# A decoder layer in fp32 products of split operands: the last output part rebuilt, copies of x shared out, and two attention-side products put in another order

## The chip, the cores and the metric

The kernel runs on one core of one Trainium2 chip. The metric is the device time of one execution in microseconds (us), lower being better. TensorE is called PE here, VectorE DVE, ScalarE ACT, GpSimd POOL and SyncE SP; PEld is PE's weight loading.

## The reference

One decoder layer on x of 512 rows by 1024, with a memory of 256 rows:

```python
x = x + 0.5 * swiglu(rms_norm(x, norm_ffn1_w), ffn1_w_in, ffn1_w_out)     # "ffn1", d_ff 2816
x = x + hybrid_mixer(rms_norm(x, norm_mix_w), ...)   # SSD scan heads + differential attention
x = x + memory_cross_attention(rms_norm(x, norm_cross_w), rms_norm(mem, norm_mem_w), ...)
x = x + 0.5 * swiglu(rms_norm(x, norm_ffn2_w), ffn2_w_in, ffn2_w_out)     # "ffn2"
return rms_norm(x, norm_final_w)

def swiglu(h, w_in, w_out):
    gate, up = jnp.split(h @ w_in, 2, axis=-1)
    return (jax.nn.silu(gate) * up) @ w_out
```

Two inner products matter below. In the differential attention the weights `w = softmax0 - lam * softmax1` are multiplied by the values, one head at a time (`po` in the kernel). In the scan the decayed products of a chunk are `y_diag` and `y_off` (`pf`, then `py` in the kernel). Both sums and products are over fp32 data.

## The kernel before, in words

**Split operands.** Every fp32 operand of a large product is split into a high and a low half. ACT copies the high half (line 155, tiles `wh`, `s31h` and so on), DVE subtracts it from the operand to get the low half (line 156, `wl`, `s31l`). A product is then three matmuls: high by high, low by high, high by low. The line numbers 155 and 156 are those of the helper, so they are the same for all tiles.

**The two feed-forward parts** use a Strassen-like scheme: for a block of four quarters, seven products instead of eight, on sums S1 to S4 of the quarters. The sums of the activations are built in `block_sums` (lines 212 to 214): `s` (the sum s31), then two half-width subtractions and additions that make the sum s24 of it, then the splits. The output product (`out_blocks`, from line 1285) runs in three sets over the 22 blocks of d_ff: 6, 8 and 8 for the first layer part. A set runs seven products of 24 matmuls of 128x512: `11` into `oa`, S1 into `oe` (these two in turn, part by part), S2 into `ob`, `12` into `oa`, S3 into `ob`, S4 into `oe`, `22` into `ob`. Each needs two parts of weights, 128x1024 each. Where the product's weights are themselves sums of quarters, the sum is made on the chip: a fetch (SP) and an accumulating DMA (POOL, line 1345), or an addition on DVE (line 1355, `t2`).

The third set of ffn1 is built with `by_dma`: its weight sums come in while the set runs. Its second product (`oe`) needs S1's weight parts and `s31l`. Next to it in PE's order stands `prel`, two 256-wide products of the relative-position bias, whose result ACT copies (`hot`, line 640) and stores by two DMAs of its own queue (`rel_d`, line 643).

**What sets the order.** SP and POOL work in the order in which the program writes their instructions. The order of ACT, DVE and PE comes from a scheduler; in the program, `Order` steps through generators whose `yield` values are the time until the next piece is due, and `behind(...)` holds an instruction after named others. Every queue then runs in order: an instruction that waits holds all behind it.

**Buffers.** Fetched weights (`wr`) have six buffers, high and low halves (`wh`, `wl`) three each. The eight PSUM banks are `acc` (4) and `aux` (4).

**Other places.** `turn` (line 1249 on) transposes four tiles of x on PE into four banks (`pxf`) and copies each back on ACT (line 1258), between ffn1 and the mixer. `memory_in` (line 1069) splits the memory's tiles (`hm`). `head` computes `po`, and `group` computes `pf` and `py`.

Of the kernel before, what the change touches and what calls it, by code (L numbers as in the profile page):

```python
# [11 lines left out]
F32 = mybir.dt.float32  # L12
R32 = mybir.dt.float32r
AF = mybir.ActivationFunctionType
ALU = mybir.AluOpType
# [85 lines left out]
def body(tc, a, dbg=None):  # L101
# [37 lines left out]

    last, start, last_sum, recent, newest, newest_mm, first_block = [], [], [], [], [], [], []  # L140
    V, S, G = nc.vector, nc.scalar, nc.gpsimd
# [63 lines left out]
    def sums_in_steps(b11, b21, b22, b12, pair=None):  # L205

        s31, s24 = s2("s31"), s2("s24")
        if pair is None:
            V.tensor_tensor(s31[:, :H], b11, b21, ALU.subtract)
            V.tensor_tensor(s31[:, H:], b21, b22, ALU.subtract)  # L210
        else:
            V.tensor_tensor(halves(s31), *pair, ALU.subtract)  # L212
        V.tensor_tensor(s24[:, :H], s31[:, H:], b11, ALU.subtract)
        V.tensor_tensor(s24[:, H:], s24[:, :H], b12, ALU.add)  # L214
        s31 = split("s31", s31)
        yield
        s24 = split("s24", s24)
        lo, hi = slice(0, H), slice(H, T)
        yield {S3: hl(s31, lo), S1: hl(s31, hi), S2: hl(s24, lo), S4: hl(s24, hi)}
# [546 lines left out]
    def head(hd, q, kq, bias):  # L766
# [69 lines left out]
        po = aux("po")  # L836
        for j in range(4):
            mm3(po[:, j * P :], v[j], (w0[j], w1[j]), j == 0, j == 3, wc=hs)
        w0.clear()
# [87 lines left out]
    def group(g, bt, ct, xs, zs):  # L927
# [52 lines left out]
        for j in range(2):  # L980
# [14 lines left out]
            with behind(list(newest_mm)):  # L995
                for c in range(1, 4):
                    mm(pf[:, c * P : (c + 1) * P], st[c - 1][:, j * P : (j + 1) * P], ct[:, c * P : (c + 1) * P], True, True)
                for c in range(4):
                    for hh in range(2):
                        pp = slice(64 * hh, 64 * hh + 64)  # L1000
                        mm(py[pp, c * P : (c + 1) * P], xdt[c // 2][:, c % 2, (2 * j + hh) * 64 : (2 * j + hh + 1) * 64], rs[hh][:, c], True, True)
# [67 lines left out]
    def memory_in(dst):  # L1069
        yield 9.0  # L1070
        for k in range(KT):
            mk = mem[k // 2][:, k % 2]
            with behind(recent):
                dst.append(split("hm", mk, par[:, C_MEM + k : C_MEM + k + 1], True))
            yield 2.0
        mem.clear()
        both = small("nboth", 4, bufs=2)[:, :2]
        V.tensor_tensor(both, msq[:, :2], msq[:, 2:], ALU.add)
        yield from st_mem.from_sums(both, 10.0)
# [171 lines left out]
    def turn(n, banks=None, summed=False):  # L1251
# [5 lines left out]
        for tb in range(4):  # L1257
            S.activation(x[4 * n + tb], pt[tb], AF.Copy)
            if summed:
# [27 lines left out]
    def out_blocks(blocks, sums, g, col4, ncol4, each=None, finale=None, clean=True, n=None, by_dma=False):  # L1287
# [13 lines left out]

        def weights(of, part, raw=None):
            if raw is None:
# [3 lines left out]
            lo = wp.tile([P, w], R32, tag="wl", name=nm("wl"))  # L1307
            recent[:] = [i.ins for i in split_into(hi, lo, raw)]
            return hi, lo
# [12 lines left out]
        def product(ps, of, which, first=False, ready=None, after=((), ())):  # L1322
            for part in parts:
                if ready and part == parts[0]:
                    w = ready
                else:
# [26 lines left out]
        def t2(part):  # L1353
            more = fetch(blocks[B22], part)
            V.tensor_tensor(t_raw[part], t_raw[part], more, ALU.add)
            return t_raw[part]
# [10 lines left out]

        later = {}
        here = sums is None
        if here:  # L1370
            sums = [t1, added(blocks[B12], blocks[B22], "gate"), t2, lambda part: t_raw[part]]
        ready = [None, None]
        if early:
            ready = [weights(of, parts[0]) for of in (blocks[B11], sums[0])]
            yield
        bank = [acc, aux]
# [5 lines left out]
        both = [product(a_ps, blocks[B11], "11", True, ready[0]), product(e_ps, sums[0], S1, True, ready[1], ((), tuple(first_block)))]  # L1382
        for _ in parts:
# [23 lines left out]
        for n, _ in enumerate(product(b_ps, sums[1], S3, after=(copies, ()))):  # L1407
            if n == 0:
                first_split = list(recent)
            elif n == 12 and by_dma:  # L1410
                with behind(first_split):
                    for part in t_raw:
                        t4(part)
            yield
        for t in range(2):
# [181 lines left out]
```

## Time and profile before

| | us |
|---|---|
| time, median of 3 runs (1299.22 to 1300.01) | 1299.35 |
| profiled execution: its own time | 1299.78 |
| profiled execution: span | 1298.0 |
| PE busy | 1284.4 |
| PEld busy | 1125.5 |
| DVE busy | 970.5 |
| ACT busy | 710.2 |
| POOL busy | 119.1 |
| third output set of ffn1, first product to last | 300.04 to 342.49 |
| transposes of x after it (`pxf`) | from 342.49 |

PE is busy for nearly the whole span, so time is only to be had where PE stands idle or runs below its usual pace: the list of waits gives the first, the start times of neighbouring matmuls in the timeline the second. In a timeline row, the first number is the start, the second the time from the start to the end of the row's group, `x4` the number of instructions in the group, and the brackets hold the idle time before it with what ended it. Rows of matmuls overlap by some tenths, since their ends are modelled. In rows of the windows view the columns are the stretch, its length, busy time of PE, PEld, DVE, ACT and POOL (with instructions), then the granted clock of PE as a share of full speed, the share of time of the DMA engines, and GB/s.

### The profile page before, as it was taken

To read this page: it belongs to the slowest core of one execution; us is meant where nothing else is said; L and a number is where in the kernel's file an instruction comes from. 1 tells how busy PE (TensorE), PEld (TensorE's weight loads), DVE (VectorE), ACT (ScalarE), POOL (GpSimd) and SP (SyncE) were. 2 spreads that over 40 slices of the span, in tenths; PEclk is the share of its full clock that TensorE was granted. 3 is DMA by queue.
4 is the path that set the end of the run, shared out by engine and by line. 5 is a ranking of instruction groups with operands and counts; after the bars stand their busy time and mean duration, and the time that the engine had idled before them with its cause. 6 is when DMAs were issued, how large, how long until landed. Compare 5 with 4: busy or idle time off the path is not lost.

```text
span 1298.0 us, 20081 instructions
## 1 busy us (share of the span) xinstructions
PE 1284.4 (99%) x7709; PEld 1125.5 (87%) x7709; DVE 970.5 (75%) x1543; ACT 710.2 (55%) x1207; POOL 119.1 (9%) x149
## 2 busy tenths in 40 slices
PE   9999999999999999999999999999999999999997
PEld 7889998998888778877888888889899899989995
DVE  6988897797776676567867696645678878877886
ACT  7544564565654564346644574434466546555554
POOL 1001010001101011100102011020001000000000
PEclk9999999999999999999999999999999999999999
DMA  9468777777975436653475567693249876666662
GB/s 336 101 172 209 183 195 207 227 192 203 295 234 155 131 65 159 227 165 98 106 207 180 158 163 223 198 228 113 66 130 249 214 223 183 185 191 191 173 206 94
DMA packets 69264, 234.75 MB, mean 181 GB/s; under 512 B 8161, under 2 KB 9665, under 8 KB 68817
## 3 DMA queue, kind: packets, MB, share of 16 engines
q1 hardware_dynamic: 53200, 180.91, 41.8%
q0 software_dynamic: 13168, 45.67, 19.8%
q10 hardware_dynamic: 2800, 6.91, 1.6%
q8 instruction: 60, 0.98, 0.3%
q14 instruction: 36, 0.29, 0.1%
HBM read 231.30 MB, written 48.29 MB: 215 GB/s over the span
## 4 chain that ended last, share of the span: by engine, by line
PE 81%; issue 12%; DMA 2%; DVE 2%; POOL 1%; ACT 1%; POOLq 0%; SPq 0%; ACTq 0%; DVEq 0%
PE qb L242 11%; PE pm L146 10%; PE qe L242 8%; PE qa L242 8%; PE pxbc L146 5%; PE ob L1319 5%; PE oa L1319 4%; PE pcq L146 3%; PE oe L1319 3%; PE pz L146 3%; PE pk L146 2%; PE pq L146 2%; PE pa L146 2%; PE pcv L146 2%; PE pv L146 2%
## 5 line engine op out<-in xcount | busy, mean ns | idle before, releaser
L155 ACT ACTIVATE wh<-wr 128x1024 fp32r<-128x1024 f32 (+1 forms) x323 | 328.2, 1018 | 304.6 <-PE qe L242 37.2
L156 DVE TENSOR_TENSOR wl<-wr,wh 128x1024 fp32r<-128x1024 f32 (+1 forms) x323 | 378.4, 1175 | 99.7 <-ACT wh L155 73.0
L788 ACT ACTIVATE ec<-ec,mn 128x512 f32<-128x512 f32 (+3 forms) x64 | 35.4, 554 | 22.0 <-DVE mn L787 22.0
L787 DVE CUSTOM_DVE_ANT_0 ec<-ps,bias 128x512 f32<-128x512 f32 (+3 forms) x64 | 28.1, 487 | 16.1 <-PE ps L146 15.9
L900 DVE SCALAR_TENSOR_TENSOR conv<-pxbc,par,conv 128x511 f32<-128x511 f32 (+2 forms) x48 | 35.7, 744 | 3.5 <-ACT conv L896 2.9
L251 POOL DMA_DIRECT2D wr<-in_f2q x11 | 9.7, 879 | 307.7 <-DMA wr<-in_f2q 116.8
L366 POOL TENSOR_TENSOR ncol<-nv,mhalf 128x4 f32<-128x4 f32 (+1 forms) x9 | 11.0, 1222 | 291.1 <-DVE nv L364 291.1
L146 PE MATMUL pxbc<-hnl,wh 128*128 128x512 f32 x128 | 35.6, 404 | 0.0
L146 PE MATMUL pxbc<-hnh,wh 128*128 128x512 f32 x128 | 35.3, 400 | 0.0
L146 PE MATMUL pxbc<-hnh,wl 128*128 128x512 f32 x128 | 32.3, 393 | 0.0
L453 DVE TENSOR_TENSOR gate<-qb,row 128x512 f32<-128x512 f32 x19 | 13.1, 692 | 22.1 <-PE qb L242 22.1
L146 PEld LDWEIGHTS pxbc<-hnh,wl 128*128 128x128 f32 x128 | 23.8, 188 | 5.3 <-issue 0.2
L251 POOL DMA_DIRECT2D wr<-in_f1q x16 | 14.0, 873 | 152.2 <-DMA wr<-in_f1q 58.9
L146 PEld LDWEIGHTS pxbc<-hnl,wh 128*128 128x128 f32 x128 | 23.2, 188 | 4.7 <-issue 0.4
L146 PEld LDWEIGHTS pxbc<-hnh,wh 128*128 128x128 f32 x128 | 23.0, 189 | 4.6 <-issue 0.5
L454 ACT ACTIVATE gate<-gate 128x1024 f32<-128x1024 f32 x19 | 20.1, 1057 | 10.9 <-DVE gate L453 10.9
L146 PE MATMUL pv<-wh,hnh 128*128 128x512 f32 x64 | 25.3, 395 | 0.0
L146 PE MATMUL pv<-wh,hnl 128*128 128x512 f32 x64 | 25.2, 393 | 0.0
L855 POOL TENSOR_TENSOR rr<-ev,mhalf 128x4 f32<-128x4 f32 x8 | 8.3, 1034 | 163.1 <-DVE ev L853 163.1
L155 ACT ACTIVATE s31h<-s 128x512 fp32r<-128x512 f32 x30 | 18.7, 624 | 7.4 <-DVE s L212 4.4
L155 ACT ACTIVATE s24h<-s 128x512 fp32r<-128x512 f32 x30 | 18.8, 625 | 7.0 <-DVE s L214 7.0
L301 ACT ACTIVATE u<-qb 128x512 f32<-128x512 f32 x19 | 11.4, 598 | 19.8 <-PE qb L242 19.8
(461 smaller groups left out, 3527.9 us busy)
## 6 DMA issues: line engine op xcount, KB each, us to landing
wr<-in_f2q SPq DMA_DIRECT2D x44, 512.0 KB, 4.4
wr<-in_f1q SPq DMA_DIRECT2D x40, 512.0 KB, 4.3
wr<-in_f1b SPq DMA_DIRECT2D x25, 512.0 KB, 5.3
isum<-in_f2q SPq DMA_DIRECT2D x22, 512.0 KB, 5.4
wr<-isum SPq DMA_DIRECT2D x22, 512.0 KB, 4.2
wsum<-in_f2b SPq DMA_DIRECT2D x20, 512.0 KB, 6.3
wr<-wsum SPq DMA_DIRECT2D x20, 512.0 KB, 4.4
wr<-in_f1q POOLq DMA_DIRECT2D x16, 512.0 KB, 6.5
```

The source lines that it names most:

```text
L146: newest_mm[:] = [nc.tensor.matmul(out, w, x, start=start, stop=stop).ins]
L155: S.activation(hi, src, AF.Copy),
L156: V.tensor_tensor(lo, src, hi.bitcast(F32), ALU.subtract),
L242: newest_mm[:] = [nc.tensor.matmul(out, w_[:, wc], xs[kp][which][x_], start=first and j == 0 and f == 0 and kp == 0, stop=j == 2 and kp == ...
L251: last_sum[:] = [G.dma_start(raw, m, accum_op=ALU.add).ins]
L301: copy = S.activation(u2, b_ps, AF.Copy)
L453: V.tensor_tensor(gate[:, 2 * i : 2 * i + 2], halves(gs[i]), row, ALU.mult)
L454: S.activation(gate, gate, AF.Silu)
L787: V.tensor_tensor_reduce(out=ec[:, :n], in0=ps[c][:, parts[i]], in1=bias[:, T - n :], scale=0.125, scalar=3e38, op0=ALU.add, op1=ALU.min, ...
L788: S.activation(ec[:, :n], ec[:, :n], AF.Exp, bias=mn, scale=-1.0, accum_out=sm[c][:, i : i + 1])
L900: V.scalar_tensor_tensor(y[:, d:], ps[:, : T - d], par[:, cw + j : cw + j + 1], y[:, d:], ALU.mult, ALU.add)
L1319: newest_mm[:] = [nc.tensor.matmul(ps, a_[:, ts], b_[:, ws], start=first and k == 0 and j == 0, stop=k == n - 1 and j == 2, skip_group_che ...
```

## The change

It has six parts.

1. In every set, the low split of the first part of S2's weights is held behind the low split of s31 (`sums_low`); all of S2's weight splits are written ahead of the copies of `oa` into `ob` (line 1392 before), and in the third set the updates of x from `oe` come behind those splits.
2. In the third set (`by_dma`) the new `ask_early` fetches B11's and S1's second part, then B22 in four 128x512 pieces named `more` (two 128x1024 fetches before), and then both parts of S3, first the `wr` buffer and then the spare `gate`, ahead of B21. The two DVE additions of t2 become four of 128x512. The accumulating DMAs of t4 go out half way through product `12` and not S3's.
3. `memory_in` starts later: its first yield is 13, not 9.
4. In `turn`, when called with banks of its own, the odd tiles' copies of x go to DVE (4 of 8).
5. In `head` the order is all `(high value, first weights)`, all `(low value, first weights)`, all `(high value, second weights)`, the last in the order 1, 2, 3, 0; before, the three stood together per tile.
6. In `group` the two halves of `py` come in the order (1, 0), not (0, 1).

```diff
@@ block_sums
         s31 = split("s31", s31)
+        sums_low[:] = last[1:]
         yield
         s24 = split("s24", s24)
@@ head
-        for j in range(4):
-            mm3(po[:, j * P :], v[j], (w0[j], w1[j]), j == 0, j == 3, wc=hs)
+        for n, (v_, w_) in enumerate(((0, w0), (1, w0), (0, w1))):
+            for j in (0, 1, 2, 3) if n < 2 else (1, 2, 3, 0):
+                mm(po[:, j * P :], v[j][v_][:, hs], w_[j], n + j == 0, n == 2 and j == 0)
@@ group
-                    for hh in range(2):
+                    for hh in (1, 0):
@@ memory_in
-        yield 9.0
+        yield 13.0
@@ turn
         for tb in range(4):
-            S.activation(x[4 * n + tb], pt[tb], AF.Copy)
+            if banks and tb % 2:
+                V.tensor_copy(x[4 * n + tb], pt[tb])
+            else:
+                S.activation(x[4 * n + tb], pt[tb], AF.Copy)
@@ weights
-            recent[:] = [i.ins for i in split_into(hi, lo, raw)]
+            high = S.activation(hi, raw, AF.Copy)
+            with behind(low_behind):
+                low = V.tensor_tensor(lo, raw, hi.bitcast(F32), ALU.subtract)
+            recent[:] = [high.ins, low.ins]
@@ t2
-            more = fetch(blocks[B22], part)
-            V.tensor_tensor(t_raw[part], t_raw[part], more, ALU.add)
+            more = pieces.pop(part) if part in pieces else (fetch(blocks[B22], part),)
+            n = t_raw[part].shape[1] // len(more)
+            for i, m in enumerate(more):
+                V.tensor_tensor(t_raw[part][:, i * n : (i + 1) * n], t_raw[part][:, i * n : (i + 1) * n], m, ALU.add)
@@ out_blocks
+        def ask_early():
+            for of, make in ((B11, lambda part: fetch(blocks[B11], part)), (S1, t1)):
+                asked[of, parts[1]] = make(parts[1])
+            for part in parts:
+                pieces[part] = [s2("more") for _ in range(*part)]
+                for k, m in zip(range(*part), pieces[part]):
+                    nc.sync.dma_start(m, blocks[B22][:, k * T : (k + 1) * T])
+            for part in parts:
+                asked[S3, part] = seventh(part)
...
         u2 = []
+        third = {part: weights(sums[2], part, low_behind=() if n else sums_low) for n, part in enumerate(parts if by_dma else parts[:1])}
+        third_split = list(recent) if by_dma else []
         for t in range(2):
             S.activation(b_ps[t], a_ps[t], AF.Copy)
-        for t in range(2):
-            update(t + 2, 1, e_ps[t], 1, False)
-        yield from product(b_ps, sums[2], S2)
+        with behind(third_split):
+            for t in range(2):
+                update(t + 2, 1, e_ps[t], 1, False)
+        yield from product(b_ps, sums[2], S2, ready=third)
...
-        yield from product(a_ps, b21 if here and not by_dma else blocks[B21], "12")
+        for n, _ in enumerate(product(a_ps, b21 if here and not by_dma else blocks[B21], "12")):
+            if n == 12 and by_dma:
+                for part in t_raw:
+                    t4(part)
+            yield
```

How this stands in the engines' order, at three places of the third set of ffn1. First ACT, from the high half of S1's second weights to the splits after `hot`, before the change (`wh` first is S1's second part, `wh` second is S2's first part):

```order
L155 ACTIVATE wh_3462<-wr_3459 128x1024
L155 ACTIVATE s31h_3396<-s_597_3391 128x512
L155 ACTIVATE wh_3495<-wr_3373 128x1024
L155 ACTIVATE s24h_3400<-s_598_3392 128x512
L1392 ACTIVATE ob_3412<-oa_3408 128x512
L1392 ACTIVATE ob_3413<-oa_3409 128x512
L155 ACTIVATE gh_3404<-th_3381 128x512
L640 ACTIVATE hot_2459<-prel_3473 8x256
L640 ACTIVATE hot_2460<-prel_3473 8x256
L643 DMA rel_d<-hot_2459 8x256
```

and after it:

```order
L1313 ACTIVATE wh_3476<-wr_3410 128x1024
L155 ACTIVATE s31h_3396<-s_597_3391 128x512
L155 ACTIVATE s24h_3400<-s_598_3392 128x512
L155 ACTIVATE gh_3404<-th_3381 128x512
L1421 ACTIVATE ob_3431<-oa_3427 128x512
L1421 ACTIVATE ob_3432<-oa_3428 128x512
L641 ACTIVATE hot_2459<-prel_3487 8x256
L641 ACTIVATE hot_2460<-prel_3487 8x256
L644 DMA rel_d<-hot_2459 8x256
L644 DMA rel_d<-hot_2460 8x256
L1313 ACTIVATE wh_3501<-wr_3373 128x1024
L1313 ACTIVATE wh_3507<-wr_3410 128x1024
```

The high half of S2's first part (`wh_3495`, now `wh_3501`) moved from the third row of the first list to behind the copies of `oa`, both `hot` copies and both DMAs.

DVE at the same place, before:

```order
L156 TENSOR_TENSOR wl_3463<-wr_3459,wh_3462 128x1024
L213 TENSOR_TENSOR s_598_3392<-s_597_3391,th_3381 128x256
L1355 TENSOR_TENSOR wr_3373<-wr_3373,wr_3492 128x1024
L214 TENSOR_TENSOR s_598_3392<-s_598_3392,th_3381 128x256
L156 TENSOR_TENSOR s31l_3397<-s_597_3391,s31h_3396 128x512
L1355 TENSOR_TENSOR wr_3459<-wr_3459,wr_3516 128x1024
L156 TENSOR_TENSOR s24l_3401<-s_598_3392,s24h_3400 128x512
L156 TENSOR_TENSOR wl_3496<-wr_3373,wh_3495 128x1024
L156 TENSOR_TENSOR gl_3405<-th_3381,gh_3404 128x512
```

and after:

```order
L1315 TENSOR_TENSOR wl_3477<-wr_3410,wh_3476 128x1024
L213 TENSOR_TENSOR s_598_3392<-s_597_3391,th_3381 128x256
L214 TENSOR_TENSOR s_598_3392<-s_598_3392,th_3381 128x256
L156 TENSOR_TENSOR s31l_3397<-s_597_3391,s31h_3396 128x512
L156 TENSOR_TENSOR s24l_3401<-s_598_3392,s24h_3400 128x512
L156 TENSOR_TENSOR gl_3405<-th_3381,gh_3404 128x512
L1365 TENSOR_TENSOR wr_3373<-wr_3373,more_3413 128x512
L1365 TENSOR_TENSOR wr_3373<-wr_3373,more_3414 128x512
L1365 TENSOR_TENSOR wr_3410<-wr_3410,more_3417 128x512
L1365 TENSOR_TENSOR wr_3410<-wr_3410,more_3418 128x512
L1315 TENSOR_TENSOR wl_3502<-wr_3373,wh_3501 128x1024
```

The 128x1024 addition that stood between the sums and `s31l` is behind it now, in four pieces, and with it the other addition.

SP, the fetches of the third set from S1's second part (`wr_3459`, now `wr_3410`) on, before (`wr_3492` and `wr_3516` are B22, `wr_3544` and `wr_3568` B21, `wr_3591` and `gate` S3):

```order
L1299 DMA wr_3459<-in_f1b 128x1024
L1299 DMA wr_3492<-in_f1b 128x1024
L1299 DMA wr_3516<-in_f1b 128x1024
L1299 DMA wr_3544<-in_f1b 128x1024
L1299 DMA wr_3568<-in_f1b 128x1024
L1299 DMA wr_3591<-in_f1b 128x1024
L1299 DMA gate_3617<-in_f1b 128x1024
```

and after:

```order
L1304 DMA wr_3410<-in_f1b 128x1024
L1386 DMA more_3413<-in_f1b 128x512
L1386 DMA more_3414<-in_f1b 128x512
L1386 DMA more_3417<-in_f1b 128x512
L1386 DMA more_3418<-in_f1b 128x512
L1304 DMA wr_3421<-in_f1b 128x1024
L1304 DMA gate_3424<-in_f1b 128x1024
L1304 DMA wr_3553<-in_f1b 128x1024
L1304 DMA wr_3574<-in_f1b 128x1024
```

S3's two fetches moved ahead of B21's two, and B22 comes in four pieces.

More of the change, by code (lines that the diff above doesn't have):

```diff
@@ L138, in dump @@
             nc.sync.dma_start(dbg[name], t.bitcast(F32) if t.dtype == R32 else t)
-    last, start, last_sum, recent, newest, newest_mm, first_block = [], [], [], [], [], [], []
+    last, start, last_sum, recent, newest, newest_mm, first_block, sums_low = [], [], [], [], [], [], [], []
     V, S, G = nc.vector, nc.scalar, nc.gpsimd
@@ L1300, in fetch, with weights @@
             return raw
-        def weights(of, part, raw=None):
+        def weights(of, part, raw=None, low_behind=()):
             if raw is None:
@@ L1323, in product @@
             for part in parts:
-                if ready and part == parts[0]:
-                    w = ready
+                if ready and part in ready:
+                    w = ready[part]
                 else:
@@ L1366, in t4, with early_or @@
             G.dma_start(t_raw[part], blocks[B21][:, part[0] * T : part[1] * T], accum_op=ALU.add)
-        later = {}
+        later, pieces, asked = {}, {}, {}
+        def ask_early():
[7 more added lines that the diff above has]
+                asked[S3, part] = seventh(part)
+        def early_or(of, make):
+            return lambda part: asked.pop((of, part)) if (of, part) in asked else make(part)
         here = sums is None
         if here:
-            sums = [t1, added(blocks[B12], blocks[B22], "gate"), t2, lambda part: t_raw[part]]
+            seventh = added(blocks[B12], blocks[B22], "gate")
+            sums = [early_or(S1, t1), early_or(S3, seventh), t2, lambda part: t_raw[part]]
         ready = [None, None]
         if early:
-            ready = [weights(of, parts[0]) for of in (blocks[B11], sums[0])]
+            ready = [{parts[0]: weights(of, parts[0])} for of in (blocks[B11], sums[0])]
             yield
+        if by_dma:
+            ask_early()
         bank = [acc, aux]
@@ L1381, in out_blocks @@
             nc.tensor.matmul(b_ps[1], ones_r, ones_r[:, None, :].to_broadcast([P, 4, P]), start=True, stop=True)
-        both = [product(a_ps, blocks[B11], "11", True, ready[0]), product(e_ps, sums[0], S1, True, ready[1], ((), tuple(first_block)))]
+        both = [product(a_ps, early_or(B11, lambda part: fetch(blocks[B11], part)) if by_dma else blocks[B11], "11", True, ready[0]), product(e_ps, sums[0], S1, True, ready[1], ((), tuple(first_block)))]
         for _ in parts:
@@ L1406, in out_blocks @@
             update(t, 0, a_ps[t])
[L1407 to L1414, printed above, removed]
+        yield from product(b_ps, sums[1], S3, after=(copies, ()))
         for t in range(2):
```

## The prediction

> **What bounds the kernel now.** I read the head of the page first, then the list of waits of PE, then the start times in the timelines where those waits lie.
>
> ```profile
> span 1298.0 us, 20081 instructions
> PE 1284.4 (99%) x7709; PEld 1125.5 (87%) x7709; DVE 970.5 (75%) x1543; ACT 710.2 (55%) x1207; POOL 119.1 (9%) x149
> ...
> PE oe L1319 <- DVE s31l L156: 1.6, 2, 1.3
> ...
> PE pck L146 <- ACT x L1258: 0.5, 1, 0.5
> ```
>
> PE is busy for 1284.4 of 1298.0 us, and the change leaves its number of matmuls as it is. So it can only gain what PE loses between matmuls. The list of waits (total, times, longest) names two places that the change touches, and a third comes below; the largest is 1.3 us in the third output set of ffn1, in `oe`, for DVE's `s31l`. The chain of waits shows what made it late.
>
> ```profile
> 296.85 9.27 DMA wr<-in_f1b
> ...
> 306.22 1.07 ACT wh L155
> ...
> 307.31 1.23 DVE wl L156
> 308.54 0.34 DVE s L213
> 308.87 1.14 DVE wr L1355
> 310.01 0.34 DVE s L214
> 310.35 0.60 DVE s31l L156
> ```
>
> The accumulating DMA of S1's second part took 9.27 us and landed at 306.12. Behind it come ACT's high half, DVE's low half, and then the sums, with a 1.14 us addition among them that nothing needs yet.
>
> ```profile
> 309.13 0.61 PE L1319 MATMUL oe<-wh,s31l 128*128 128x512 f32 x2
> 311.00 0.50 PE L1319 MATMUL oe<-wh,s31l 128*128 128x512 f32 x1 [1.26 <-DVE s31l L156]
> 311.43 1.02 PE L146 MATMUL prel<-hot,rel_sb 32*8 32x256 f32 x4
> 312.39 0.50 PE L1319 MATMUL oe<-wh,s31l 128*128 128x512 f32 x1
> 312.73 1.42 PE L1319 MATMUL oe<-wl,s31h 128*128 128x512 f32 x4
> ```
>
> The row of two at 309.13 would be followed at 309.59 (2 x 0.227 us from the neighbouring rows' spacing, four in 0.907: for instance `oe` before it). The third matmul began at 311.00, so 1.41 us are lost. The windows show a second price.
>
> ```profile
> 309.92:313.33 3.41, 2.33 (x9) 1.24 (x10) 3.41 (x6) 3.21 (x6) 0.00 (x0) 1.00 0.61 162
> 313.33:316.74 3.41, 3.41 (x10) 2.65 (x9) 3.41 (x7) 3.33 (x7) 1.56 (x3) 0.50 0.68 220
> ...
> 344.05:347.46 3.41, 2.85 (x24) 2.36 (x22) 2.22 (x7) 3.41 (x9) 1.49 (x2) 1.00 0.95 363
> ```
>
> In the stretch with the stall PE was busy for 2.33 of 3.41 us; in the next the granted clock was 0.50. Ten matmuls started there, where 3.41 / 0.227 = 15 fit; with those that lie across its ends I count 7 slowed ones, at 0.2 us more each 1.4 us, and set the price at half of 3.41 less what the half-started ones keep, 1.6. The stretch around the `pxf` copies (2.85 busy) was followed by none.
>
> **The change part by part.** Part 1 and 2, the third set. The 1.14 us addition goes from before `s31l` to behind it. If the DMA lands at 306.12 as now, `s31l` ends 310.95 - 1.14 = 309.81, 0.2 late. It should land sooner: before the change, SP issued B22 and B21 on both sides of it, and now the four pieces and S3's first part stand ahead of it in time. I take 303 to 304.5, which gives 307.8 or so, before 309.59: no wait here, 1.41 gained.
>
> But the stall moves on. ACT's high half of S2's first part, `wh`, stood ahead of the copies of `hot`; now it stands behind them, and `hot` waits for `prel` on PE.
>
> ```profile
> 310.12 1.06 ACT L155 ACTIVATE wh<-wr 128x1024 fp32r<-128x1024 f32 x1 [2.32 <-DVE wr L1355]
> ...
> 313.12 0.62 ACT L640 ACTIVATE hot<-prel 8x256 f32<-8x256 f32 x2
> 313.50 0.27 ACTq L643 DMA_DIRECT2D rel_d<-hot  x1
> 313.82 0.51 ACT L159 ACTIVATE hm<-mem,par 128x256 fp32r<-128x256 f32 x1
> ```
>
> Without the wait, PE runs its third `s31l` product at 309.59, `prel` from 309.82 to 310.78 (312.39 less 311.43 is 0.96), and five matmuls more, 1.13, so that `ob` is wanted at 311.91. ACT can start `hot` at 310.87, is through with both and the DMA after 0.70 (313.12 to 313.82) and up to 0.27 more for the second DMA, and needs 1.06 for `wh`: 312.63 to 312.90, so `ob` begins 0.7 to 1.1 late. I take 1.0, with ends 0.5 and 1.5. What waits behind it on ACT is only the second part's half, wanted half a product later. So the third set gains 1.41 - 1.0 = 0.4 (-0.1 to 0.9), and not the 1.4 that the wait's row promises.
>
> The slowed clock. With 1.0 us of idle the busy share of a window is some 0.3 us larger than before. One window of 2.33 busy was followed by half clock and one of 2.85 wasn't; the new one lies between, nearer the latter if the pause falls across the end of a window, which no row can tell. I take the 1.6 as gained, at three chances in four. [...]
>
> Other fetches: on SP, S3's two parts go past B21, and the second waits for the `gate` buffer, which the last quad of the input product has read by about the time this set is under way (an estimate: 304 to 305). B21 follows it. Even with ten us to land (S1's accumulation took 9.27) and 1.06 and 1.23 for its halves it is ready by 317.5; product `12` needs it after `ob`'s 24 matmuls, 312.9 + 24 x 0.227 = 318.3. So I cost this at nothing, with cover of about 1 us then and more if it lands sooner; each us beyond is one of PE. The smaller DVE additions sum to the same time. The t4 accumulations, now one product earlier, wait for nothing on PE's path.
>
> Part 1 in ffn2's first set:
>
> ```profile
> 1028.67 0.61 PE L1319 MATMUL oe<-wh,s31h 128*128 128x512 f32 x2
> 1029.63 0.73 PE L1319 MATMUL oe<-wh,s31l 128*128 128x512 f32 x2 [0.34 <-DVE s31l L156]
> ...
> 1027.75 1.23 DVE L156 TENSOR_TENSOR wl<-wr,wh 128x1024 fp32r<-128x1024 f32 x1 [0.26 <-ACT wh L155]
> 1028.89 0.69 DVE L156 TENSOR_TENSOR s31l<-s,s31h 128x512 fp32r<-128x512 f32 x1
> ```
>
> `oe` was due at 1028.67 + 0.45 = 1029.12 and came at 1029.63. With `s31l` ahead of the 1.23 us `wl` it is done by 1028.9. Gain 0.5; the `wl` that is now later has half a microsecond of cover (its product comes after both of `oe` and `oa`).
>
> Part 4 and 3, the turn.
>
> ```profile
> 342.49 3.68 PE L150 MATMUL pxf<-ident,x 128*128 128x128 f32 x32
> 346.26 0.50 PE L146 MATMUL nrow<-ndiag,ones_r 128*128 128x256 f32 x2
> 347.24 2.18 PE L146 MATMUL pck<-hm,wh 128*128 128x256 f32 x16 [0.47 <-ACT x L1258]
> ...
> 344.40 1.21 DVE L156 TENSOR_TENSOR wl<-wr,wh 128x1024 fp32r<-128x1024 f32 x1
> ```
>
> `pck` needs a bank that the fifth ACT copy of x frees. In the new order `pck` follows `pxf` at once and waits for a DVE copy instead, queued behind that `wl`: it ends near 345.55 + 0.65 = 346.2 (0.65 by DVE's 128x512 rows, 0.69 above). So `pck` starts near 346.3, and the two `nrow` (0.24) come later: 347.24 - 346.3 - 0.24 = 0.7. The norm's sums stand behind DVE's copies now, so the wide `nrow` may come 0.1 to 0.2 late. I take 0.55 (0 to 0.7).
>
> Part 5, `po`.
>
> ```profile
> 641.52 0.88 PE L146 MATMUL po<-wt,vh 128*128 128x512 f32 x2
> 642.24 0.40 PE L146 MATMUL po<-wt,vl 128*128 128x512 f32 x1
> ```
>
> Two matmuls took 0.72 where 0.45 is usual: the second waited for a low half of the weights that the new order wants eight matmuls later. That is 0.27; at the other heads only a few hundredths per head are to be seen. I take 0.3 (0 to 0.6).
>
> Part 6, `py`. The scheduler had split the group, the first `py` ahead of two other products and the rest behind.
>
> ```profile
> 685.47 0.83 PE L146 MATMUL pf<-th,st 128*128 128x128 f32 x6
> 686.23 0.43 PE L146 MATMUL py<-th,xdt 128*64 128x128 f32 x2
> 686.59 0.74 PE L146 MATMUL pxbc<-hnh,wh 128*128 128x512 f32 x2
> 687.26 1.09 PE L146 MATMUL py<-th,xdt 128*64 128x128 f32 x14
> ...
> 747.19 0.43 PE L146 MATMUL py<-th,xdt 128*64 128x128 f32 x2 [0.17 <-DVE th L992]
> ```
>
> The two `py` took 0.36 where a sixteenth of a whole group (16 in 1.02) is 0.06 each, and the two `pxbc` 0.67 for 0.45: about 0.45 lost by changing over twice. In the new order all `py` stand together. In the later group the same split goes, but the wait comes again in another form, since its first `py` now needs the other half of `th`. I take 0.45 for both (0 to 0.65).
>
> Sum: 0.4 + 1.6 + 0.5 + 0.55 + 0.3 + 0.45 = 3.8. The profiled execution took 1299.78, 0.43 above the median; taken from the median the forecast is 1299.35 - 3.8 = 1295.55, say 1295.6.
>
> **The rivals.** The slow clock stays: the pause before `ob` falls into a low window again, or the slow stretch has a cause other than PE's idleness and comes in any case. For it: 2.33 against 2.85 leaves the point open, and 1.26 us of idleness is little to halve a clock. Then 3.8 - 1.6 = 2.2, and 1297.2. [...]
>
> The stall vanishes altogether, since `hot` costs ACT less than the rows say or `prel` runs earlier: 1.4 + 1.6 + 1.8 for the rest = 4.8, and 1294.5. Against it: `hot` can't start before `prel`'s end.
>
> The small parts come to little: the waits removed show up at the next matmul. With a third of them and no better clock it is 1298.6.
>
> Slower: S1's accumulation lands late, since four pieces and S3's part, 1.5 MB, are queued just ahead of it. Every us past 305.9 is a us of PE, as wh, wl, two sums and `s31l` take 3.7 us in a row; the slow clock then stays. Against the other gains of 1.8 and the third set's 3.0 it decides from 309.1 on, a transfer of 12.3 us, and 1302 needs 15.
>
> ```profile
> gate<-in_f1b POOLq DMA_DIRECT2D x1, 512.0 KB, 11.5
> ```
>
> The longest such transfer in that stretch took 11.5, so 12.3 isn't out of reach, but 15 is.
>
> **How the numbers follow.** Forecast 0.50 (own range 1294.6 to 1296.6); slow clock stays 0.25; no stall 0.12; small parts fail 0.08; slower 0.05. About 0.2%, 2.6 us, is what a measurement of this kernel can tell from none: faster is below 1296.75. The forecast gives 0.46 of that, no stall 0.12, the slow clock 0.05: faster 0.63. The rest of them with the failed small parts is 0.32, slower 0.05. Range 1294.0 to 1298.6: it leaves out the slower case, and a little of the forecast's and the no-stall case's better end.
>
> **What would show it.** In the profile after: no wait of `oe` for `s31l` at 309 or 1029; the list of waits with a new row of about 1.0 for `ob` at `wh`, with ACT's `hot` ended just before it; a granted clock of 1.00 in every window after 306. At the turn `pck` right behind `pxf` with a DVE copy as its releaser, and less than 0.3 us of loss. No gap inside `po` at 641 and unsplit `py` rows. I would be wrong if the accumulation still lands at 306 or later, if the wait before `ob` is 1.5 us or none, if a window shows 0.50 again, or if B21's high half comes late for `12`.

## The result and the profile after

The changed kernel's median is 1295.43 us (1294.53 to 1296.80, 8 runs), that of the kernel before 1299.31 us (1298.11 to 1300.86, 8 runs) beside it. The ratio is 0.9972 with a 95% interval of 0.9964 to 0.9981: faster by 3.9 us, 0.28%. The forecast was 1295.6. Measured once more beside the kernel before (`after_again` below), the ratio was 0.9981 (0.9972 to 0.9989).

The head of the page of the changed kernel, and from its list of waits of PE (total, times, longest) the rows of this chapter:

```profile
span 1294.1 us, 20089 instructions
PE 1281.5 (99%) x7709; PEld 1123.7 (87%) x7709; DVE 971.9 (75%) x1549; ACT 707.6 (55%) x1203; POOL 118.0 (9%) x149
...
PE ob L1327 <- ACT wh L1313: 0.9, 1, 0.9
PE po L146 <- ACT wt L155: 0.4, 1, 0.4
...
PE py L146 <- DVE th L994: 0.2, 1, 0.2
```

The wait of `oe` for `s31l` is gone, both of them, and so is that of `pck`. In their place stands the wait of `ob` for `wh`. The chain of waits there reads as follows (start, length, what):

```profile
308.99 1.59 PE oe L1327 x7
310.57 0.97 PE prel L146 x4
311.54 0.02 issue
311.56 0.65 ACT hot L641 x2
...
312.28 0.31 ACTq L644
312.59 0.05 issue
312.63 1.06 ACT wh L1313
```

PE's own `prel` holds ACT's `hot`, then come two DMAs of ACT's queue and `wh`. In the timeline of PE:

```profile
313.74 1.20 PE L1327 MATMUL ob<-wh,s24h 128*128 128x512 f32 x4 [0.86 <-ACT wh L1313]
...
341.10 3.65 PE L150 MATMUL pxf<-ident,x 128*128 128x128 f32 x32
344.51 2.16 PE L146 MATMUL pck<-hm,wh 128*128 128x256 f32 x16
...
684.33 1.09 PE L146 MATMUL py<-th,xdt 128*64 128x128 f32 x16
...
745.84 1.09 PE L146 MATMUL py<-th,xdt 128*64 128x128 f32 x16 [0.16 <-DVE th L994]
...
1024.99 0.62 PE L1327 MATMUL oe<-wh,s31h 128*128 128x512 f32 x2
1025.45 0.63 PE L1327 MATMUL oe<-wh,s31l 128*128 128x512 f32 x2
```

`pck` follows `pxf` without a wait, both groups of `py` are whole, and `oe` in ffn2 goes on in 0.46 us.

Since both kernels have the same number of matmuls on PE, the two profiles can be held against each other matmul by matmul: the n-th of one against the n-th of the other, at places where the order is the same in both. The difference of the start times then grows or shrinks only where something is lost or gained. That account, in us against the profile of before (minus is a gain), for every kernel profiled here:

| profile | sets 1 and 2 | third set | turn | `po` | first `py` | second `py` | ffn2's first set |
|---|---|---|---|---|---|---|---|
| changed kernel | 0.00 | -1.99 | -1.05 | -0.17 | -0.55 | -0.57 | -0.61 |
| after_again | 0.00 | -1.99 | -1.08 | -0.17 | -0.55 | -0.61 | -0.61 |
| prel_early | +1.64 | -2.20 | -1.13 | -0.14 | -0.55 | -0.57 | -0.64 |
| act_copies | 0.00 | -2.01 | -1.13 | -0.12 | -0.55 | -0.58 | -0.62 |
| t4_late | 0.00 | -1.93 | -1.12 | -0.13 | -0.55 | -0.61 | -0.62 |
| hot_six | +1.17 | +1.09 | -1.09 | -0.18 | -0.55 | -0.58 | -0.61 |
| prel_hold | +0.63 | -1.08 | -1.05 | -0.14 | -0.55 | -0.61 | -0.61 |
| not_early | +1.62 | +4.84 | -0.41 | -0.13 | -0.55 | -0.61 | -0.61 |
| memory_9 | 0.00 | -0.57 | -0.88 | -0.16 | -0.55 | -0.61 | -0.62 |
| small_only | +1.04 | -2.63 | +0.40 | -0.16 | -0.55 | -0.57 | -0.61 |
| before_py | 0.00 | -1.59 | -0.03 | +0.06 | -0.55 | -0.59 | 0.00 |
| before_low | 0.00 | -1.06 | -0.03 | +0.01 | 0.00 | -0.02 | -0.62 |
| before_mem13 | 0.00 | -1.11 | +0.25 | +0.08 | 0.00 | -0.01 | -0.01 |

The sum of the first row is -4.9; the very first matmuls came 0.6 later in this execution than in that of before, and a late fetch at 1058 cost 0.37, which leaves the -3.9 between the spans. The starts alone differ by up to 1.3 us between executions (-0.5 to +0.8 against before).

### The profile page after: what moved, and what is told of

The parts are those of the page before. It is cut to its first block, busy times and chain, and to the rows that moved or that the text cites. A ratio compares the mean times of both kernels' runs of the same rounds, so it can differ in the third digit from the quotient of the medians.

```text
span 1294.1 us, 20089 instructions
## 1 busy us (share of the span) xinstructions
PE 1281.5 (99%) x7709; PEld 1123.7 (87%) x7709; DVE 971.9 (75%) x1549; ACT 707.6 (55%) x1203; POOL 118.0 (9%) x149
## 4 chain that ended last, share of the span: by engine, by line
PE 82%; issue 12%; DMA 2%; ACT 1%; DVE 1%; POOL 1%; POOLq 0%; SPq 0%; ACTq 0%
PE qb L243 12%; PE pm L146 10%; PE qe L243 8%; PE qa L243 8%; PE pxbc L146 5%; PE ob L1327 5%; PE oa L1327 4%; PE oe L1327 4%; PE pcq L146 3%; PE pz L146 3%; PE pa L146 2%; PE pk L146 2%; PE pq L146 2%; PE pcv L146 2%; PE pv L146 2%
## 5 line engine op out<-in xcount | busy, mean ns | idle before, releaser
L788 DVE CUSTOM_DVE_ANT_0 ec<-ps,bias 128x512 f32<-128x512 f32 (+3 forms) x64 | 28.1, 486 | 14.8 <-PE ps L146 14.7
```

What stands on the lines that cost most here:

```text
L788: V.tensor_tensor_reduce(out=ec[:, :n], in0=ps[c][:, parts[i]], in1=bias[:, T - n :], scale=0.125, scalar=3e38, op0=ALU.add, op1=ALU.min, ...
```

## The experiments

Each kernel was profiled once, the changed one twice; where a ratio is given, it was also timed in rounds beside the kernel before. The last five columns of the table hang on the order alone: where the order is the same they repeat to within 0.1 us, so a single profile shows them. The first two depend on when transfers land and differ from execution to execution (sets 1 and 2 from 0.00 to +1.64).

**Is it `hot` that now holds `ob`?** prel_early asks for `prel` 3 us sooner, so that `hot` stands ahead on ACT:

```diff
         V.memset(rel_far, MASKED)
-        yield 9.0
+        yield 6.0
```

> The changed kernel with prel due 3 us earlier (its first yield 6 and not 9), so that both hot copies stand ahead of the copies of oa on ACT and only those stand between them and S2's first high half. If the 0.86 us wait of ob for wh in the changed kernel is due to hot waiting for prel, then wh runs from about 311.1 (when the first two pieces are added, 311.0) to 312.1, ahead of ob at 312.7: no wait, 0.8 to 1.0 us less than the changed kernel, about 1294.5, ratio near 0.9965. Rival, that the four additions on DVE or their pieces set it: the wait stays at 0.5 or more, and the time within 0.4 of the changed kernel's.

Measured: ratio 0.9978 (0.9967 to 0.9988), no better than the changed kernel. In its profile, the accumulation of S1's second part from the chain of waits, and then rows of the timelines of DVE, ACT and PE:

```profile
298.96 8.27 DMA wr<-in_f1b
```

```profile
312.54 2.49 DVE L1365 TENSOR_TENSOR wr<-wr,more 128x512 f32<-128x512 f32 x4
...
313.86 2.27 ACT L1313 ACTIVATE wh<-wr 128x1024 fp32r<-128x1024 f32 x2 [0.28 <-DVE wr L1365]
...
314.97 1.21 PE L1327 MATMUL ob<-wh,s24h 128*128 128x512 f32 x4 [0.63 <-ACT wh L1313]
```

The accumulation landed at 307.23, 5.1 us into the set; in the first profile of the changed kernel it landed at 303.01, 2.4 us into it. Behind it the chain wh, wl, two sums, three low halves and only then the additions is so long that S2's first `wh`, from 313.86 to 314.92, waits for the first two of the four additions instead of for `hot`. The wait is 0.63, not 0.86 and not 0: with a late landing the rival holds, that the additions set it. Whether the wait would be gone after an early landing stays open. A second thing is in this profile: the second set lost 1.6 us, at `oe` for `s31l` (0.41 idle) and at `ob` (0.53 idle) with the matmuls around them, where ten of the fourteen profiles lose nothing.

**Holding the addition back in the other sets too.** prel_hold has the same `yield 6.0`, and in the sets without `by_dma`:

```diff
             for i, m in enumerate(more):
-                V.tensor_tensor(t_raw[part][:, i * n : (i + 1) * n], t_raw[part][:, i * n : (i + 1) * n], m, ALU.add)
+                with behind(() if by_dma or part != parts[0] else sums_low):
+                    V.tensor_tensor(t_raw[part][:, i * n : (i + 1) * n], t_raw[part][:, i * n : (i + 1) * n], m, ALU.add)
```

> The changed kernel with prel due 3 us earlier, as in prel_early, and in the sets without by_dma the addition that makes S2's first part held behind the low split of s31 (in the second set it stands between the two steps of the sum s24 now). Theory: what spreads the executions is when S1's accumulations land; where they land late, the second set loses up to 1.4 us at oe and ob, and the third keeps a wait of 0.6. With the addition behind it, the second set loses 0.2 at most even with a late landing, and the third 0 (early) to 0.6 (late). Against the changed kernel, run beside it: 0.7 to 1.7 us less, near 1294 with 1295.2 for that. Rival, that the addition is only late elsewhere: a wait of ob for S2's first high half of 0.5 or more in a set that has none now, and no gain.

> The changed kernel itself once more, for a second profile and time beside prel_hold. Steps of the account that come from the order of PE repeat within 0.05 us: turn -1.1, po -0.15, py -1.1, ffn2's first set -0.6 against the kernel before. Steps that hang on a landing (second set, third set) may differ by up to 1.5. Ratio near 0.9972.

Measured side by side: prel_hold 0.9982 (0.9973 to 0.9990), the changed kernel 0.9981 (0.9972 to 0.9989). No gain, where 0.7 to 1.7 us were expected. prel_hold's profile lost 0.6 in the first set. There `ob` waits for the `wh` of S3, whose accumulating DMA went out at 81.85 against 77.82 in after_again: the addition is late elsewhere, as the rival has it, though at another product than the rival named. In the third set it shows:

```profile
298.31 9.38 DMA wr<-in_f1b
...
312.99 2.50 DVE wr L1366 x4
```

```profile
315.42 0.96 PE L1327 MATMUL ob<-wh,s24h 128*128 128x512 f32 x3 [1.79 <-ACT wh L1313]
```

The landing came at 307.68 here, 6.3 us into the set, and the wait is 1.79; in prel_early it came 5.1 us into the set, and the wait is 0.63. So neither is a version that beats the changed kernel. The repeated columns of after_again came out as expected, within 0.06; its ratio was expected near 0.9972.

**Do the shared copies gain at the turn?** act_copies puts all eight on ACT again, memory_9 keeps the sharing and takes the later start of `memory_in` back:

```diff
-            if banks and tb % 2:
+            if False:
```
```diff
     def memory_in(dst):
-        yield 13.0
+        yield 9.0
```

> The changed kernel with all eight copies of x in the turn on ACT again; PE's order is the same as in the changed kernel. If it is the sharing of the copies that gains at the turn, pck starts late again: 0.5 to 1.1 us of the 1.1 that the turn gained are lost. Rival, that the turn gains by PE's order (pck before nrow, in a bank that the first odd copy frees, and not the last one): ACT's second copy ends by 344.3 and pck starts at 344.5 as before; lost is at most 0.3, at the high half of the next weights, which ACT makes after four more copies.

> The changed kernel with memory_in's first yield 9 again; DVE keeps its four copies of x in the turn, but PE's order there is that of before (nrow ahead of pck). If only the order gains, the turn's step is -0.3 or less. If the shared copies would have been enough by themselves: the second odd copy, which frees pck's bank here, ends at 344.7, when nrow is through, and the step is -0.9 or more.

Measured: -1.13 at the turn without the sharing, -0.88 without the later start. The timeline of PE, of act_copies and then of memory_9:

```profile
341.11 3.65 PE L150 MATMUL pxf<-ident,x 128*128 128x128 f32 x32
344.52 0.72 PE L146 MATMUL pck<-hm,wh 128*128 128x256 f32 x4
```

```profile
342.06 3.65 PE L150 MATMUL pxf<-ident,x 128*128 128x128 f32 x32
345.47 0.48 PE L146 MATMUL nrow<-ndiag,ones_r 128*128 128x256 f32 x2
345.92 0.95 PE L146 MATMUL pck<-hm,wh 128*128 128x256 f32 x6
```

So either of the two edits is enough here. The order of PE (`pck` ahead of `nrow`) comes from `memory_in`, and in it `pck` needs a bank that the second copy frees, whoever makes it. memory_9's profile also shows the third set's `ob` waiting 1.72, since a split of the memory (ACT at 311.68, DVE at 312.20) now stands between the additions there.

**Is it t4's accumulations that let DVE come in time?** t4_late has them half way through S3's product again.

```diff
-        for n, _ in enumerate(product(a_ps, b21 if here and not by_dma else blocks[B21], "12")):
-            if n == 12 and by_dma:
+        for n, _ in enumerate(product(b_ps, sums[1], S3, after=(copies, ()))):
+            if n == 0:
+                first_split = list(recent)
+            elif n == 12 and by_dma:
```

> The changed kernel with t4's accumulations half way through S3's product again, not product 12. If these, landing earlier, are what lets DVE come to the turn's copies sooner (its last low half of the set began 3.1 us earlier), then at the turn DVE's updates wait for that low half again, the copy that frees pck's bank ends 0.6 later or more and pck starts 0.2 to 0.5 late. Rival, that they do nothing at the turn: no difference over 0.1 at pck.

Measured: -1.12 at the turn, third set -1.93. They do nothing there. The rival held.

**What is the early fetching worth?** not_early leaves only the call out.

```diff
-        if by_dma:
-            ask_early()
```

> The changed kernel without ask_early: S3 and B22 are fetched in the old order, B22 as two 128x1024, and the orders of DVE and ACT at the third set fall back to those before (the addition between the two sums, S2's first high half ahead of hot). If part 2 removes the wait of oe for s31l, it comes back here with 1.0 to 1.5 us, the wait of ob for wh (0.86) goes, and the slow clock comes or not with where the stretch falls: 0.4 more than the changed kernel, or 1.8. Rival, that the two waits had other causes: no wait at oe, or both.

Measured: 1304.43 in one run, some 6 us above the median of before beside it (1298.05), and neither theory had it. There is no wait of `oe` in the third set and none of `ob` for S2's `wh`, but one of 6.1 us at S3's product. The chain of waits and the windows (stretch, length, PE, PEld, DVE, ACT, POOL, clock, DMA share, GB/s):

```profile
316.31 0.09 POOL wr L1376
...
316.89 13.33 DMA wr<-in_f1b
...
330.31 1.07 ACT wh L1313
```

```profile
324.56:327.97 3.41, 0.74 (x4) 0.28 (x2) 0.00 (x0) 0.00 (x0) 0.00 (x0) 1.00 1.05 275
327.97:331.38 3.41, 0.00 (x0) 0.00 (x0) 0.00 (x0) 1.07 (x2) 0.00 (x0) 0.50 1.04 272
331.38:334.80 3.42, 3.38 (x8) 2.71 (x9) 1.62 (x2) 1.38 (x3) 0.00 (x0) 0.50 0.75 199
```

On POOL the two t4 accumulations (L1376) now stand ahead of S3's (L1353), which therefore was issued at 316.89 (305.12 in the changed kernel) and took 13.33 us beside them. So two edits of part 2 hang together: with t4 moved ahead, S3 must be asked for early. The other way round it isn't so, as t4_late shows.

**Does PE's idleness slow its clock?** hot_six makes the first `hot` copy six times over, the same result each time:

```diff
         for i in range(2):
-            S.activation(hot[i][:8], prel[:, i * H : (i + 1) * H], AF.Copy, scale=-8.0)
+            for _ in range(1 if i else 6):
+                S.activation(hot[i][:8], prel[:, i * H : (i + 1) * H], AF.Copy, scale=-8.0)
```

> The changed kernel with the first hot copy made six times over (the same result each time), which holds ACT for 5 x 0.31 = 1.5 us more ahead of S2's first high half. The wait of ob grows from 0.86 to about 2.2. If little matmul work in a stretch of 3.41 us slows the clock of the next, a stretch with granted clock 0.50 comes after it, unless the wait lies across the end of a stretch: 1.3 for the wait and 1.4 to 1.6 for the clock, nearly 3 us in all. Rival, that a wait of 1 to 2 us slows no clock and the slow stretch before the change had another cause: clock 1.00 throughout and 1.3 us.

Measured: the wait is 2.34, and a stretch at half clock follows; the third set is at +1.09, which is 3.1 us more than the changed kernel's. From its timeline of PE and its windows:

```profile
316.05 1.35 PE L1328 MATMUL ob<-wh,s24h 128*128 128x512 f32 x4 [2.34 <-ACT wh L1314]
317.19 1.91 PE L1328 MATMUL ob<-wh,s24l 128*128 128x512 f32 x4
```

```profile
313.55:316.96 3.41, 1.07 (x5) 0.78 (x5) 1.69 (x3) 3.31 (x8) 0.00 (x0) 1.00 1.00 335
316.96:320.37 3.41, 3.41 (x10) 2.64 (x9) 3.41 (x6) 1.73 (x3) 2.50 (x3) 0.50 1.08 221
```

PE was busy for 1.07 of 3.41 us, and the next 3.41 us ran at 0.50. Of the 3.1 us, 1.5 is the longer wait (2.34 against 0.86) and 1.6 the slow clock, by the start times of the matmuls. So here a wait slowed the clock, from 1.00 to 0.50. And since `hot`, held 1.5 us longer, holds `ob` 1.5 us longer, it is `hot` that sets the start of `ob` in the changed kernel.

**The small parts without the third set**, and three of them each by itself on the kernel before: small_only has `memory_in`, the shared copies, `po`, `py` and the held low split; before_py, before_low and before_mem13 have one edit each. Their edits are those of the diff of the change, but for the low split:

```diff
-        yield from product(b_ps, sums[2], S2)
+        yield from product(b_ps, sums[2], S2, low_behind=sums_low)
```

> The kernel before with parts 3, 4, 5 and 6 and the low split held behind s31's (part 1's first half), but with the third set of ffn1 as before: no early fetches, t4 late, S2's high half ahead of hot. By the account of the profiles these parts are worth 1.1 + 0.15 + 1.1 + 0.6 = 2.95 in every execution: ratio near 0.9977, a little over the changed kernel's if the third set's rebuilding gains the rest (2.0 in the first pair of profiles, with 1.4 of it for the slow clock). In its third set: a wait of oe for s31l of 0 to 1.3, no wait of ob. Rival, that the rebuilt set is worth nothing on the mean over executions (its own wait of ob takes 0.9 to 1.9): the same ratio as the changed kernel, within 0.0005.

> The kernel before with the order of py's halves alone changed (12 rows of PE differ, in two groups). If splitting the group is the cost, both groups gain 0.55: 1.1 against the kernel before between the two ends of the scan, and the 0.17 wait for th stays. Rival, that only the first gains: 0.55 and nothing.

> The kernel before with only the first low split of S2's weights held behind s31's low split; its orders differ on DVE (8 rows) and ACT (2 rows) in ffn2's three sets alone. If the 0.34 wait of oe there came from the 1.23 us low split ahead of s31l: 0.6 less over ffn2's first set and no change elsewhere but for the start and the landings. Rival, that a later edit did it: no gain there.

> The kernel before with memory_in's first yield 13 alone; all copies of x stay on ACT. PE's order at the turn becomes the changed kernel's (pck ahead of nrow). If that order alone gains what the turn gains: 1.1 less there. Rival, that it needs the shared copies: 0.5 or less.

Measured: `py` alone gains 0.55 and 0.59, and its wait stays; the low split alone gains 0.62 in ffn2 and nothing elsewhere. Both as their theories had it. From the timelines of PE, of before_py and of before_low:

```profile
684.89 1.09 PE L146 MATMUL py<-th,xdt 128*64 128x128 f32 x16
...
746.41 1.09 PE L146 MATMUL py<-th,xdt 128*64 128x128 f32 x16 [0.16 <-DVE th L992]
```

```profile
1027.36 0.62 PE L1323 MATMUL oe<-wh,s31h 128*128 128x512 f32 x2
1027.82 0.63 PE L1323 MATMUL oe<-wh,s31l 128*128 128x512 f32 x2
```

small_only came to 0.9989 (0.9980 to 0.9998), 1.4 us and not 3, and less than the changed kernel's 0.9972 and 0.9981, though the intervals overlap. Its turn loses 0.40, and before_mem13's 0.25, against both theories. From the timeline of small_only:

```profile
341.16 2.13 PE L150 MATMUL pxf<-ident,x 128*128 128x128 f32 x18
343.58 0.33 PE L150 MATMUL pxf<-ident,x 128*128 128x128 f32 x1 [0.30 <-DVE x L1344]
344.24 1.64 PE L150 MATMUL pxf<-ident,x 128*128 128x128 f32 x13 [0.33 <-DVE x L1344]
346.06 2.14 PE L146 MATMUL pck<-hm,wh 128*128 128x256 f32 x16 [0.19 <-DVE x L1261]
```

Now `pxf` itself waits for the last updates of x on DVE, which come late: the last low split ahead of them ends 1.7 us after the set's end, here and in before_mem13. In before_py, without the later `memory_in`, it ends 0.7 us after it and `pxf` doesn't wait. In the changed kernel the same updates begin as the set ends. Since before_mem13 has the later `memory_in` as its only edit and the same two waits of `pxf`, that edit brings them. That it does so by two more of the memory's splits ahead of the low split on DVE is read from the order. So the turn's 1.1 us need the rebuilt set as well as one of the two edits. In this profile the account to the right of the third set is +0.40 - 0.16 - 0.55 - 0.57 - 0.61 = -1.5, which is about the time measured.

These four are also four more executions of the old third set. None has a stretch at half clock. They wait for `s31l` there 0.64 (before_py), 0.81 (before_low), 0.33 (before_mem13) and not at all (small_only, which had lost 1.0 in the second set). And they wait at a place where the first profile had nothing to speak of, S3's second part in `ob`, for 0.2 to 0.8, here in before_low and before_mem13:

```profile
327.41 1.21 PE L1323 MATMUL ob<-wh,s31h 128*128 128x512 f32 x4 [0.69 <-ACT wh L1309]
```

```profile
328.43 1.21 PE L1319 MATMUL ob<-wh,s31h 128*128 128x512 f32 x4 [0.77 <-ACT wh L155]
```

## Why the prediction was right, and where it was not

The total was right: 3.8 forecast, 3.9 and in the second comparison some 2.5 (0.19% of 1298) measured, and the sign and range with it. The account of the first pair of profiles bears out the largest block too, 0.4 + 1.6 = 2.0 for the third set against 1.99. But the steps inside are only partly right.

- **The stall moves to `ob`.** Right, in place, mechanism and size: 1.0 forecast, idle 0.86 (1.03 between the starts) by the chain of `prel`, `hot`, two DMAs and `wh`, which hot_six bears out. In the four profiles with just this order on ACT it was 0.86 to 0.9. In the others, with `hot` or the memory's splits moved, the additions hold `wh` where the landing is late, and it is up to 1.8.
- **"It should land sooner."** In the profile of the changed kernel it did, at 303.01, but not as a rule. From the start of the set to the landing of S1's accumulation it took 6.1, 5.5, 5.6, 5.2, 2.8 and 1.5 us with the old order of the fetches (before, before_py, before_low, before_mem13, small_only, not_early), and 2.4, 5.2, 4.3, 5.3, 5.9, 5.1, 6.3 and 5.2 with the new one (changed, after_again, act_copies, t4_late, memory_9, prel_early, prel_hold, hot_six). No effect of the order shows in that. The wait of `s31l` is gone in all eight even so. By the order of DVE the reason is the 1.14 us addition that no longer stands ahead of it: in memory_9, with a landing 5.9 us into the set, PE didn't wait there. No run tried that by itself. It was in the working, as the case of an unchanged landing with 0.2 left. (In prel_early, prel_hold and hot_six something else differs too; in the first two `prel` stands earlier in PE's order, so that `s31l` is wanted later by the 0.97 us of `prel`.)
- **"I take the 1.6 as gained, at three chances in four."** The mechanism was right and the weight wrong. In hot_six a wait of 2.34 us was followed by half clock, while with the changed kernel's 0.86 the clock stayed at 1.00. But of five executions of the old third set, one had the slow stretch, the profiled one. Its price was right too, 1.6 by the start times of the matmuls, but as a regular gain it was worth a fraction of that. The profiled execution's own time, 1299.78 against a median of 1299.35, had room for that reading.
- **The third set in the usual execution.** Three old executions that had lost nothing in the second set stand at -1.06, -1.11 and -1.59 by the account, the new set at -2.0: it gains 0.4 to 0.9 there, where 0.4 was forecast without the clock. Part of that is the wait at S3's second part, which the first profile did not show and which is gone in the changed kernel.
- **Turn: 0.55 forecast, 1.05 to 1.13 measured**, outside its bounds (0 to 0.7). `pck` was expected at 346.3 in the old times, behind a `wl` and a DVE copy; it started at 344.51, which is 345.9 in those times, with no wait at all. The step took DVE's place in the queue from the old profile, while in the rebuilt set the last low split began 3.1 us sooner (338.82 against 341.93), 1.7 beside PE. It gave the credit to the shared copies; either they or the later memory splits do it, and both only together with the rebuilt set.
- **`py`: 0.45 for both forecast, 1.12 to 1.16 measured**, outside its bounds (0 to 0.65). The first group's 0.45 was right (0.55). For the second I let the wait for `th` eat the gain. The wait is as long as before, 0.16 against 0.17, and the split cost 0.55 there too.
- **`po`: 0.3 forecast, 0.12 to 0.18 measured**, inside its bounds. **ffn2: 0.5 forecast, 0.61 measured.**
- **B21 behind S3 at no cost** held: no profile of the changed order waits for `12`'s weights.

Taken over executions the sum is some 0.7 (third set) + 1.1 + 0.15 + 1.15 + 0.6 = 3.7: as large as the forecast, but without the 1.6 for the clock, and with 0.55 more at the turn, 0.7 more at `py`, 0.3 more in the third set and 0.1 more in ffn2, less 0.15 at `po`. That the total was hit owes something to errors that cancel, and so is in part luck. The second comparison gave 2.5 (1.4 to 3.6), a little less than this sum; what is missing there was not found.

On the rivals: "no stall" did not come: in no run with the new third set did `ob` start in time. "The slow clock stays" had the right reason in part, since a longer wait left the clock alone where a shorter one was followed by half clock: before's 1.26 us, 1.08 of it in one stretch of 3.41 and with 0.96 of `prel` beside it, was followed by 0.50, and prel_hold's 1.79, with 1.15 us idle in one stretch, was followed by full clock. "Slower" did not come in the changed kernel, but not_early shows that its kind was near: an accumulation of 13.33 us, S3's and not S1's, longer than the 12.3 from which it was to decide, stood there behind two others on POOL. The prediction's reading that 11.5 us was the longest such transfer, and 15 out of reach, was wrong: in the profile of before the two t4 accumulations, issued at 316.59 and 317.96, took 14.7 and 18.2 us to land.

## What to carry to other kernels

One profile is one execution: of five executions of the old third set the wait for `s31l` behind S1's landing was 1.26, 0.81, 0.64, 0.33 and 0 us, and the slow clock behind it was there in one, so a sum built on one profile should carry such terms with their odds and not in full. Waits that come from an order (a group split in two, a copy that stands ahead of a needed one) repeated here to within 0.1 us (the last five columns of the account, where the order is the same), and an account of start times, matmul by matmul, shows them down to the 0.12 us of `po`. A gain at one place can belong to another edit: the turn's gain vanished, and turned to a loss, without the rebuilt set before it.

## What the runs showed of the hardware that was not expected

The clock: the stretches at half clock began at whole multiples of 3.413 us after the start of the first full clock that the trace of the same execution records (in before 313.33 and 6.13, so 307.20 us or 90 of them; 91 in hot_six, 94 in not_early), and lasted one such stretch in before and hot_six and two in not_early. Counting in such stretches by the windows view, PE idled in the one ahead for 1.08 us (that much of the wait of 1.26 lay in it) with 0.96 of the narrow `prel` beside it (before), for 2.34 (hot_six), and for 2.67 and then all 3.41 (not_early). No half clock followed 0.81 with 0.96 of `prel` (before_low), 0.74 with 0.96 (memory_9), nor 1.15 (prel_hold). The last stretches of the executions fit in: 1.96 idle was followed by half clock (t4_late), 1.46 was not (hot_six). From before_low and t4_late:

```profile
309.34:312.76 3.42, 2.61 (x11) 1.35 (x11) 3.42 (x5) 3.33 (x7) 0.00 (x0) 1.00 0.61 186
312.76:316.17 3.41, 3.41 (x17) 2.82 (x16) 3.41 (x7) 3.33 (x7) 2.02 (x3) 1.00 0.76 208
```

```profile
1282.19:1285.61 3.42, 1.46 (x7) 0.88 (x5) 3.10 (x8) 2.42 (x6) 0.80 (x2) 1.00 0.69 261
1285.61:1289.02 3.41, 0.00 (x0) 0.00 (x0) 0.72 (x2) 0.98 (x2) 0.63 (x1) 0.50 0.82 307
```

Idleness alone doesn't order these cases, since 1.08 was followed by half clock and 1.46 was not. If `prel`, whose rows have 32*8 where the other matmuls' have 128*128, counts as idle, it does: of the stretches named here those with up to 1.77 us idle of 3.41 were followed by full clock, those with 1.96 and more by half clock. That `prel` counts as idle rests on the one stretch of before.

The landings: in the two profiles of the changed kernel S1's accumulating transfer of 512 KB in the third set took 8.42 and 8.35 us, but it was issued at 294.59 and at 297.64. In all fourteen profiles it took 6.1 to 10.1 us. The second set lost 1.0 to 1.6 us to a late landing in four of the fourteen profiles (prel_early, hot_six, not_early, small_only) and nothing in the others: in these four its S1 accumulation landed at 185.96 to 186.76, in the other ten at 182.09 to 184.68. A loss of that size is about half of the spread of the changed kernel's times, 2.3 us. It was not found what makes a landing early or late.
